# Operands, modulation and result additions moved in a one-core diffusion layer

## The chip, the cores and the metric

The kernel runs on 1 of the 8 cores of a Trainium2 chip. The metric is the device time of one execution in microseconds (us), lower is better. Of the kernel before there are three timed runs, and one further execution was recorded by the hardware profiler.

## The reference

One layer on 1024 latent tokens and 256 context tokens of width 1024. All is float32.

```python
x  = x  + 0.5 * ml[2] * swiglu(modulate(rms_norm(x,  norm1_g), ml[0], ml[1]), ffn1_w_in, ffn1_w_out)
cx = cx + 0.5 * mc[2] * swiglu(modulate(rms_norm(cx, norm1_g), mc[0], mc[1]), ffn1_w_in, ffn1_w_out)
hx = modulate(rms_norm(x, norm2_g), ml[3], ml[4])
hc = modulate(rms_norm(cx, norm2_g), mc[3], mc[4])
bg, cg, vc, q, k, v, gate = split(hx @ w_in)       # hc @ w_in gives keys and values of the context
y  = bg * short_conv(cg * vc, conv_w)
o  = attention(rope(norm(q)), [k_c, rope(k)], [v_c, v])
x  = x + ml[5] * ((sigmoid(gate_c) * (y @ w_bc) + sigmoid(gate_a) * (o @ w_ba)) @ w_out)
x  = x + 0.5 * ml[8] * swiglu(modulate(rms_norm(x, norm3_g), ml[6], ml[7]), ffn2_w_in, ffn2_w_out)
out = rms_norm(x, final_g)
```

The nine modulations are `ml = split(silu(c) @ w_mod + b_mod)`, and `mc` likewise from `c_ctx`. Each is a vector of 1024 numbers that needs 4 MB of `w_mod`. Modulation 5 scales the mixers' result, 6 and 7 shift and scale the third norm, and 8 scales the second FFN's result. From the fifth on only the latent ones are needed.

## The kernel before

**Numbers in two parts.** Every operand of a large product is split into a high part (ScalarE, ACT, casts it) and a low part (VectorE, DVE, subtracts the high part from the original). A product is then three matmuls: high by high, high by low, low by high (`split`, `mm3`, `terms`). So each tile of an operand costs one cast and one subtraction before TensorE (PE) can use it.

**Seven products for eight.** The large products run by Winograd's variant of Strassen's scheme. In `Winograd`, products 1, 2, 6, 7, 4, 5 and 3 are made for a pair of weight column blocks, and DVE combines their results. Each product is 12 matmuls of 128x512. Its right operands are eight sets `r[0..7]`, made from the two token halves by the norm. `norm0` makes the sets of the first half, and `norm1` makes sets 6 and 5 channel by channel and at its end keeps sets 7, 4 and 3, four casts and four subtractions each. `start` makes products 1 and 2 of the first nine pairs ahead, and `run(norm, ...)` in between draws the norm's steps. What is left of the norm is put into `self.late`, and `second` draws from it.

**Rows.** `row_products` does the FFNs' second halves in the same scheme, in the order 2, 1, 4, 6, 5, 7, 3. One product is 11 blocks of hidden rows in groups of two, each block 12 matmuls into four PSUM banks. Products 1, 6 and 7 accumulate in the same four banks (`chain`). `sums` forms the combined operands of later products behind each group, `add` (`add1`, `add3`) puts a finished product's results onto the tokens, and `after1` and `after3` are called behind each group and at the end of a product: they store the tokens, take their squares and draw steps of the next norm (`norms2`). The second FFN's last product is done in two halves of the tokens (`halves=True`).

**Modulations.** The first ones are made at the start. `later_mod` makes the others on DVE from `w_mod`: for each half of a modulation it has eight loads of 256 KB, each followed by a multiply-add into an accumulator for every stream (latent, context). Some empty steps follow, then the split of the accumulator, some more steps, and two matmuls with a column of ones that sum over the partitions. ACT copies the row, four small DMAs turn it into a column, and DVE adds the bias. It is a generator: each `yield` is a step, and the loops around it draw steps. `STEPS` says how many are drawn behind each of the first FFN's 22 column blocks, with three more for each of 12 blocks of context work at the 12th; the rest of `steps` follows at the end of that loop. `late_steps` (modulations 6, 7 and 8) are drawn in the mixers and in the second FFN.

**Mixers and merge.** The mixers loop over eight channel blocks. Each has one pair for `cg` and `vc` and one for `bg` and `gate_c`, and every second has one for `gate_a`. Then come the keys, values and queries, the attention, and the merge: `merge(j, ch)` is 24 matmuls for a block of 128 output channels and half of the tokens, 14 of them behind the attention. The product with `w_out` follows, and the second FFN.

**Order of the work.** The program is traced in order, and a scheduler then orders each engine's queue by its own estimate of when things are ready, with the earlier traced first among those that are. An instruction that is pinned (`keep_in_program_order`) stays behind the one traced just before it on its engine. Everything issued while `strict[0]` is true is pinned. The unpinned may move past it. Each engine then works its queue in the order that was fixed. Loads and stores go through the queue of SP, and a few accumulating loads through that of POOL. Small tiles of 128x512 (`ttile`, tag "t") share eleven buffers: accumulators, loaded rows of `w_mod`, sums of weights on POOL, the mixers' values, squares, head values. An instruction that needs one waits until the last user of an older one is done.

Nearly all instructions are issued by the helper in line 88, so the profile is read by the tiles' names: `r` right operands, `wl` and `wh` weights in parts, `s` sums of weights, `macc`, `acch` and `accl` a modulation's accumulator and its parts, `rawm` the rows of `w_mod`, `uc` values made ahead, `x` tokens, `hid` the FFN's hidden rows, `ga` and `z` the merge's operands, `oh` and `ol` the attention's output in parts, `xb` and `hsw` head values.

## Time and profile before

| what | value |
|---|---|
| three runs, median (lowest to highest) | 2687.64 us (2686.28 to 2688.88) |
| the profiled execution, its own time | 2688.7 us |
| its span, first to last instruction | 2686.9 us |
| mean granted TensorE clock | 0.993 |
| DVE busy | 2007.1 us (75%) |
| ACT busy | 1166.1 us (43%) |
| moved by DMA | 364.84 MB, mean 136 GB/s |

The span is the time between the first and the last instruction of the program in the trace, and 1.8 us of the execution lie around it. An engine's busy time is the union of its instructions. TensorE's matmuls overlap in the records, so its busy time says where it had nothing to do and not how fast it went; the number of matmuls in a stretch says that. The granted clock is what the throttle let TensorE have.

The work lies as follows on the span's axis: the first FFN's first half from the start to 671 us, its second half to 887, the mixers to 1287, heads and attention to 1840, the merge to 1933, the product with `w_out` to 2021, and the second FFN to the end.

### The profile page before, as it was taken

The page shows a single profiled execution, that of the slowest core. Times are in us where ns is not written, and L with a number is a line of the kernel's source. Part 1 is how long each engine was busy: PE and PEld are TensorE (multiplying, and loading weights), DVE is VectorE, ACT ScalarE, POOL GpSimd, SP SyncE. Part 2 cuts the span into 40 slices and gives each one's busy share as a digit, 9 for nine tenths or more (in the row PEclk, how much of TensorE's full clock was granted, in tenths as well). Part 3 has the DMA queues.
Part 4 walks back from the last instruction along what each step waited for, and adds up shares of the span by engine and source line. Part 5 has one row for each costly group of instructions (what it writes and reads, how often), then busy time and mean ns, then how long its engine had stood idle before and what let it go on. Part 6 is the DMA issues. An engine that isn't in the chain of part 4 may idle for free.

```text
span 2686.9 us, 37399 instructions
## 1 busy us (share of the span) xinstructions
PE 2643.4 (98%) x13593; PEld 2236.0 (83%) x13593; DVE 2007.1 (75%) x3356; ACT 1166.1 (43%) x2317; POOL 521.3 (19%) x409
## 2 busy tenths in 40 slices
PE   8999999999999999999999999999999999999998
PEld 5788898888788877888999888877888888888888
DVE  5888888786887889877488666775458875667875
ACT  6633543333454632333244666674236333334543
POOL 1244012121110044232033111000001533230200
PEclk9999999999999999999999999999999999999998
DMA  7655653346973445433213211002524543228731
GB/s 267 236 180 166 223 184 124 109 130 240 293 169 102 149 137 165 134 114 116 97 48 103 95 62 49 24 25 78 167 85 146 184 145 99 83 90 305 165 83 63
DMA packets 369920, 364.84 MB, mean 136 GB/s; under 512 B 27830, under 2 KB 261448, under 8 KB 369736
## 3 DMA queue, kind: packets, MB, share of 16 engines
q1 hardware_dynamic: 360712, 345.17, 39.0%
q0 software_dynamic: 9024, 17.30, 4.0%
q8 instruction: 106, 1.74, 0.3%
q14 instruction: 78, 0.64, 0.1%
HBM read 296.30 MB, written 66.06 MB: 135 GB/s over the span
## 4 chain that ended last, share of the span: by engine, by line
PE 88%; DVE 6%; DMA 2%; ACT 2%; issue 1%; SPq 1%; POOL 0%; DVEq 0%; ACTq 0%; POOLq 0%
PE ps L88 73%; PE po L88 7%; PE pt L88 7%; DMA rawm<-in_w_mod_dram 1%; DVE macc L88 1%; DVE wl L88 1%; SPq L88 1%; DVE xb L88 0%; DVE r L88 0%; ACT r L88 0%; DMA raw<-in_ffn_w_in_dram 0%; DMA xtok<-in_ctx_dram 0%; DVE ol L88 0%; DVE x L88 0%; DVE pts L88 0%
## 5 line engine op out<-in xcount | busy, mean ns | idle before, releaser
L88 PE MATMUL ps<-r,wl 128*128 128x512 f32 x5232 | 1213.4, 392 | 11.6 <-ACT wl L88 6.8
L88 PEld LDWEIGHTS ps<-r,wl 128*128 128x128 f32 x5232 | 983.9, 189 | 220.0 <-ACT wl L88 9.0
L88 ACT CAST wl<-s 128x512 fp32r<-128x512 f32 x256 | 158.0, 620 | 338.3 <-PE ps L88 266.6
L88 POOL TENSOR_TENSOR s<-raw 128x512 f32<-128x512 f32 x64 | 92.4, 1444 | 993.8 <-PE ps L88 346.6
L88 ACT CAST wl<-raw 128x512 fp32r<-128x512 f32 x286 | 176.4, 619 | 250.0 <-PE ps L88 160.6
L88 DVE TENSOR_TENSOR wl<-raw,wl 128x512 fp32r<-128x512 f32 x284 | 202.6, 717 | 68.3 <-ACT wl L88 64.7
L88 DVE TENSOR_TENSOR wl<-s,wl 128x512 fp32r<-128x512 f32 x256 | 231.8, 906 | 12.3 <-ACT wl L88 10.7
L88 POOL TENSOR_TENSOR s<-raw,s 128x512 f32<-128x512 f32 x64 | 99.8, 1560 | 363.9 <-DVE wl L88 354.4
L88 DVE SCALAR_TENSOR_TENSOR macc<-rawm,silu_c,macc 128x512 f32<-128x512 f32 x168 | 137.9, 837 | 9.5 <-DMA rawm<-in_w_mod_dram 9.1
L88 PE MATMUL ps<-wh,r 128*128 128x256 f32 x768 | 141.6, 285 | 0.0
L88 DVE TENSOR_TENSOR pts<-pt,pts 128x512 fp32r<-128x512 f32 x160 | 108.8, 687 | 39.4 <-ACT pts L88 38.4
L88 DVE TENSOR_TENSOR u<-u,ps 128x512 f32<-128x512 f32 x168 | 114.2, 680 | 28.5 <-PE ps L88 28.4
L88 DVE TENSOR_REDUCE m<-ps 128x1 f32<-128x512 f32 (+1 forms) x192 | 110.9, 596 | 31.0 <-PE ps L88 30.3
L88 ACT CAST pts<-pt 128x512 fp32r<-128x512 f32 x160 | 93.2, 593 | 88.7 <-PE pt L88 86.8
L88 ACT CAST rh<-hid 128x512 fp32r<-128x512 f32 x132 | 81.6, 621 | 112.2 <-PE ps L88 96.2
L88 PE MATMUL ps<-rh,wl 128*128 128x512 f32 x360 | 122.0, 389 | 0.0
L88 PEld LDWEIGHTS ps<-wh,r 128*128 128x128 f32 x768 | 120.6, 192 | 0.0
L88 ACT CAST wh<-raw 128x512 fp32r<-128x512 f32 (+1 forms) x88 | 69.3, 795 | 103.0 <-PE ps L88 79.5
L88 PE MATMUL po<-pts,vh 128*128 128x512 f32 x256 | 110.5, 437 | 1.5 <-ACT pts L88 1.5
L88 DVE TENSOR_TENSOR rl<-hid,rh 128x512 fp32r<-128x512 f32 x132 | 90.1, 686 | 26.5 <-ACT rh L88 13.5
L88 PE MATMUL ps<-wl,r 128*128 128x256 f32 x384 | 108.8, 283 | 0.0
L88 PE MATMUL ps<-kl,qs 128*128 128x512 f32 x384 | 105.3, 397 | 0.0
(298 smaller groups left out, 5068.1 us busy)
## 6 DMA issues: line engine op xcount, KB each, us to landing
raw<-in_ffn_w_in_dram SPq DMA_DIRECT2D x125, 512.0 KB
raw<-in_ffn_w_out_dram SPq DMA_DIRECT2D x72, 512.0 KB
rawm<-in_w_mod_dram SPq DMA_DIRECT2D x128, 256.0 KB
raw<-in_w_in_dram SPq DMA_DIRECT2D x61, 512.0 KB
hid<-hd SPq DMA_DIRECT2D x40, 512.0 KB
ws<-in_ffn_w_out_dram POOLq DMA_DIRECT2D x30, 512.0 KB, 6.6
ucd<-uc SPq DMA_DIRECT2D x22, 512.0 KB
hd<-c SPq DMA_DIRECT2D x38, 256.0 KB
```

Of the source, the lines that this page charges most:

```text
L88: inst = getattr(self.engine, name)(*args, **kw)
```

## The change

- **Late operands.** In the mixers' `start`, no norm step is drawn at pairs 5, 6 and 8, so operand sets 4 and 3 are still to be made when it ends. `second` makes set 4 between products 6 and 7 and set 3 behind product 4, both pinned. The line that drew `9 - self.n_ahead` steps is removed; with nine pairs made ahead it drew none.
- **Modulations.** Modulation 5 moves from the first FFN's steps to `late_steps`. These are drawn two at a time in the mixers from the fourth channel block on (30 in all, before 78), five behind each of the 14 merges (70), and the rest in the second FFN (28, before 36). The first FFN draws 154 steps in all, before 198. In `later_mod` each stream's split is followed by three steps and its own matmuls; before, all streams were split, and six steps later all were multiplied. A half of one stream has 16 steps, before 19.
- **Results.** In `row_products` a product's results are added behind the first group of the next product, pinned (unpinned in the second FFN's halves), and the call at the end of a product moves with them. Two steps of the mixers' first norm move a group later, from groups 0 and 4 to 2 and 6.

```diff
-STEPS = (0, 4, 4, 4, 5, 5, 5, 5, 5, 5, 5, 2, 12)
+STEPS = (0, 3, 3, 4, 4, 4, 4, 4, 4, 4, 4, 4, 7)
...
-            parts = []
-            for acc in accs:
+            for acc, v in zip(accs, streams):
                 ah, al = ttile("acch", dt=F32R), ttile("accl", dt=F32R)
                 split(acc, ah, al)
-                parts.append((ah, al))
-            for _ in range(6):
-                yield
-            for (ah, al), v in zip(parts, streams):
+                for _ in range(3):
+                    yield
                 mod, pm = (modl, modc)[v], ps_t()
...
-                run(norm, 2 if i == 0 else 1)
+                run(norm, 2 if i == 0 else 0 if self.plain and i in (5, 6, 8) else 1)
...
-            run(norm, 9 - self.n_ahead)
...
-            run(self.late, 4)
+            self.late_operands(1)
             dve.tensor_add(out=v, in0=u, in1=self.product(7))
...
-            run(self.late)
+            self.late_operands()
             return v, b
+
+        def late_operands(self, n=None):
+            strict[0] = True
+            run(self.late, n)
+            strict[0] = False
...
-        chain = None
+        chain, results = None, []
+
+        def add_results():
+            while results:
+                i, ps = results.pop()
+                for o, ch in to[i]:
+                    for d in range(4):
+                        add(o + d, ch, ps[d])
+                after(i, rows.n)
+
...
                 strict[0] = True
                 sums(i, g)
+                add_results()
                 strict[0] = False
                 after(i, k)
-            for o, ch in to[i]:
-                for d in range(4):
-                    add(o + d, ch, ps[d])
-            after(i, rows.n)
+            results.append((i, ps))
+        if not halves:
+            add_results()
...
                     kept.append(lr)
+                add_results()
                 after(8, k)
...
-        for m in range(2, 6):
+        for m in range(2, 5):
             yield from later_mod(m)
 
-    steps, late_steps = all_later_mods(), (step for m in (6, 7, 8) for step in later_mod(m))
+    steps, late_steps = all_later_mods(), (step for m in (5, 6, 7, 8) for step in later_mod(m))
...
-        if i == 3 and k in (0, 4):
+        if i == 3 and k in (2, 6):
             run(norms2, 1)
...
-        if i > 1:
-            run(late_steps, 5)
+        if i > 2:
+            run(late_steps, 2)
         for ch, bg, gc in mixed():
-            if i > 1:
-                run(late_steps, 4)
+            if i > 2:
+                run(late_steps, 2)
...
                 run(merge(j, ch))
+                run(late_steps, 5)
```

## The prediction

> **What bounds the kernel now.** I read the page first, then the stretches by stage, then TensorE's waits and the timelines around its gaps.
>
> ```profile
> span 2686.9 us, 37399 instructions
> PE 2643.4 (98%) x13593; PEld 2236.0 (83%) x13593; DVE 2007.1 (75%) x3356; ACT 1166.1 (43%) x2317; POOL 521.3 (19%) x409
> PE   8999999999999999999999999999999999999998
> ```
>
> TensorE is busy from end to end, and the change neither adds nor removes a matmul. So a gain can only come out of its gaps and of the time its clock was lowered. The stretches say where these lie: us, TensorE busy (matmuls), weight loads, DVE, ACT, POOL, granted clock, DMA.
>
> ```profile
> 680.00:720.00 40.00, 36.94 (x168) 30.14 (x167) 34.12 (x48) 17.75 (x31) 5.03 (x4) 1.00 0.98 317
> 720.00:930.00 210.00, 210.00 (x948) 174.45 (x947) 173.13 (x275) 108.80 (x186) 16.66 (x15) 1.00 0.54 143
> 930.00:960.00 30.00, 24.95 (x98) 20.09 (x97) 24.95 (x41) 16.80 (x34) 13.39 (x8) 0.89 0.46 150
> 1050.00:1070.00 20.00, 17.43 (x64) 13.47 (x63) 19.59 (x28) 4.93 (x9) 9.43 (x7) 0.83 0.34 110
> 1290.00:1450.00 160.00, 160.00 (x1324) 159.06 (x1324) 105.82 (x289) 65.66 (x236) 37.21 (x72) 1.00 0.19 62
> 1840.00:1930.00 90.00, 90.00 (x408) 74.55 (x407) 45.78 (x62) 22.78 (x32) 0.00 (x0) 1.00 0.43 134
> 2110.00:2410.00 300.00, 300.00 (x1325) 247.95 (x1324) 202.72 (x279) 96.08 (x160) 100.44 (x69) 1.00 0.36 113
> 2410.00:2600.00 190.00, 190.00 (x840) 157.34 (x839) 157.77 (x224) 88.63 (x154) 26.66 (x22) 1.00 0.71 197
> ```
>
> The row of 2110 is undisturbed 512-wide work: 300 / 1325 = 0.2264 us a matmul. At that rate 930:960 lost 30 - 98 x 0.2264 = 7.8 us and 1050:1070 lost 20 - 64 x 0.2264 = 5.5 us, in both with a lowered clock (0.89, 0.83). In 680:720 there are shorter matmuls too, so I take its gaps. TensorE's timeline has them, the time in brackets being idle time:
>
> ```profile
> 703.11 0.50 PE L88 MATMUL pt<-rh,wl 128*128 128x512 f32 x1 [1.39 <-ACT wl L88]
> 706.92 0.73 PE L88 MATMUL pt<-rh,wl 128*128 128x512 f32 x2 [1.67 <-DVE wl L88]
> 943.57 2.93 PE L88 MATMUL ps<-r,wl 128*128 128x512 f32 x6 [5.05 <-ACT wl L88]
> 1057.68 0.73 PE L88 MATMUL ps<-r,wl 128*128 128x512 f32 x2 [1.51 <-ACT wl L88]
> 1059.48 2.93 PE L88 MATMUL ps<-r,wl 128*128 128x512 f32 x6 [1.07 <-DVE wl L88]
> ```
>
> Three places: the turn from the first to the second product of the first FFN's output (3.06 us idle), the start of the mixers (7.8), and the mixers' ninth pair (5.5). Each one is a part of the change. Together they are 16.4 us, or 0.6% of the span. That is the ceiling of what its aims can bring.
>
> **Results a group later.** `row_products` traced the additions of a product right behind its last matmul. DVE and ACT at that turn:
>
> ```profile
> 702.44 0.62 ACT L88 CAST wl<-raw 128x512 fp32r<-128x512 f32 x1 [0.29 <-DMA raw<-in_ffn_w_out_dram]
> 701.81 2.72 DVE L88 SCALAR_TENSOR_TENSOR x<-ps,gate_l,x 128x512 f32<-128x512 f32 x4
> 704.45 1.21 DVE L88 TENSOR_TENSOR hid<-hid,hid 128x1024 f32<-128x1024 f32 x1
> 706.18 0.68 DVE L88 TENSOR_TENSOR wl<-raw,wl 128x512 fp32r<-128x512 f32 x1
> ```
>
> The first gap (1.39) ends with ACT's high part of a weight that had just landed: the DMA engines are 0.98 busy there, and the change leaves those bytes, so I leave this gap. The second ends with the low part. DVE could have made it at 703.1, but four additions (2.72 us) and a sum (1.21 us) stood ahead of it. With the additions traced behind the first group's operands this gap goes: -1.7 us. Ends: 0 (the weight's other half is late too) and -3.06. No bank is missed: the next product but one is the first to want the delayed banks, and it is a whole product away. At the later turns, in both FFNs, there is no gap to win: TensorE is busy in 210.00 of 210 us and in 190.00 of 190.
>
> Behind the seventh product more is moved: its eight additions, SP's eight stores, ACT's squares, the root for the next norm, now all pinned, and two norm steps a group later (24 matmuls, 5.4 us). What that norm feeds:
>
> ```profile
> 878.41 4.88 DVE L88 TENSOR_TENSOR x<-x,pt 128x512 f32<-128x512 f32 x8 [0.53 <-PE pt L88]
> 885.61 0.74 DVE L88 SCALAR_TENSOR_TENSOR x<-ps,gate_l,x 128x512 f32<-128x512 f32 x1
> ```
>
> It ends barely ahead of the mixers' first product, which begins about when the last results appear (885.61). If its time slid with its place, TensorE would wait up to 5.4 us. But it ran far behind its old place in the program already, held up by squares that were mixed with operands. Pinned, the squares come first, so I take 0; ends: -1 (a residue at 943 less) and +5.4.
>
> **Late operands.** Ahead of the 5.05 us gap:
>
> ```profile
> 936.17 3.74 ACT L88 CAST r<-t 128x512 fp32r<-128x512 f32 x7
> 940.29 0.62 ACT L88 CAST r<-t 128x512 fp32r<-128x512 f32 x1
> 940.82 2.18 ACT L88 CAST r<-h 128x512 fp32r<-128x512 f32 x4
> 942.89 1.14 ACT L88 CAST wl<-s 128x512 fp32r<-128x512 f32 x2
> 934.51 1.74 POOL L88 TENSOR_TENSOR s<-raw,raw 128x512 f32<-128x512 f32 x1
> 937.93 4.29 DVE L88 TENSOR_TENSOR r<-t,r 128x512 fp32r<-128x512 f32 x7
> 943.34 2.48 DVE L88 TENSOR_TENSOR r<-h,r 128x512 fp32r<-128x512 f32 x4
> ```
>
> POOL's weight sums are there at 936.3, yet ACT casts them at 942.89, behind twelve casts of right operands (eight of them r<-t). The change makes eight of the twelve, those of products 4 and 3, inside the first pair. Then ACT has four left, 4 x 3.74/7 = 2.1 us, and the weights come about 4.3 us sooner, sooner still if the norm ran ahead. TensorE went idle at 943.57 - 5.05 = 938.5 and needs a weight's low part two matmuls later, at about 939. DVE has 4 x 4.29/7 = 2.5 us of the four that stay, until 940.4, and then the low part, 0.7 us as at 706.18. So a residue of 0 to 2.1 us stays; I take 1.0, and the sum has -6.8 here. The eight that moved cost DVE 8 x 0.61 = 4.9 us in the pair's 60 matmuls (13.6 us). They are pinned behind the addition of product 6 and the subtraction of product 4, with the later additions and weight low parts of the same pair queued behind them; who waits are products 4 and 3, each a product (12 x 0.2264 = 2.7 us) or more away, with four weights made ahead. That covers it; were the cover gone, it would cost up to 2.5 us.
>
> The clock gives the residue another price. At 943 a 5.05 us gap came with 0.89 over 30 us, 3.3 us of clock; at 1057 two gaps of 1.51 and 1.07 came with 0.83 over 20 us, 3.4 us; 1.39 and 1.67 at 703 came with 1.00. So a residue of 2.1 may or may not bring some 3.3 us more: upper end 5.4. In the Trainium skill, "TensorE: Matmul & The Clock Gate", section "Why this matters for your kernels", the clock falls after idle gaps above about 3 us. By that rule the residue would cost itself alone, and the sum would be the same with 3.3 us off its upper end; the trace at 1057 disagrees, since neither gap there reaches 3 us.
>
> **Modulations.** At 1057 the chain is one of buffers:
>
> ```profile
> 1053.04 1.47 POOL L88 TENSOR_TENSOR s<-raw 128x512 f32<-128x512 f32 x1 [10.38 <-DVE accl L88]
> 1055.60 1.37 POOL L88 TENSOR_TENSOR s<-s,raw 128x512 f32<-128x512 f32 x1 [1.09 <-DMA yd<-y]
> ```
>
> POOL had data but no tile among the eleven of "t": a modulation's accumulator held one until DVE's low part. The change starts the late modulations at the fourth channel block instead of the third, two steps a time for four or five, so the first split moves to the sixth block, where no set-aside pair is fetched into these tiles any more. I take the whole 5.5; ends 0 (the same at the new place) and -5.5.
>
> In the merge 14 x 5 = 70 steps are added, at 16 a half 4.4 halves. Durations of one step (min/median/max):
>
> ```profile
> L88 DVE SCALAR_TENSOR_TENSOR macc<-rawm,silu_c,macc x168: 737/745/1821, 30.4 to 2212.2; 128x512 f32<-128x512 f32 x168
> L88 DVE TENSOR_SCALAR macc<-rawm,silu_c x24: 472/484/1524, 29.4 to 2173.2; 128x512 f32<-128x512 f32 x24
> L88 DVE TENSOR_TENSOR accl<-macc,acch x24: 679/684/1782, 42.7 to 2231.3; 128x512 fp32r<-128x512 f32 x24
> SPq L88 <- DVE wl L88: 68.2, 11, 45.0
> ```
>
> A half is 7 x 0.745 + 0.484 + 0.684 = 6.4 us of DVE, so 28 us on the 45.8 of 90: covered. POOL is empty there. On SP each half puts eight loads of 256 KB and four small ones ahead of the merge's weights, about 9.2 MB in 90 us or 102 GB/s on 134, under the 317 shown above. SP's own waits there are for weight buffers (68.2 us, last row), so it runs ahead. If a load holds SP for want of a tile, TensorE pays: 0 to 5.5 us by the row at 1050; I take 0.5, nearest to the idle DVE. In the first FFN two halves leave (12.8 us of DVE) from stretches without gaps: 0. Its other order could move the 1.13 and 1.80 us gaps below, hence -2.9 as an end. In the second FFN 28 steps stay of 36, beside full TensorE: 0.
>
> ```profile
> 277.32 0.39 PE L88 MATMUL ps<-h1ch,wl 128*128 128x256 f32 x1 [1.13 <-ACT wl L88]
> 287.43 0.51 PE L88 MATMUL ps<-h1ch,wl 128*128 128x256 f32 x2 [1.80 <-DVE wl L88]
> ```
>
> **Sum.** The profiled execution took 2688.7 us, 1.1 above the runs' median of 2687.64. 2688.7 - 1.7 - 6.8 - 5.5 + 0.5 = 2675.2; less 1.1: 2674.
>
> **Rivals.** One halving of the clock stays. With the mixers' start unchanged it is 2688.7 - 1.7 - 5.5 + 0.5 - 1.1 = 2680.9; with the ninth pair unchanged 2679.6. For it: the tile shortage is only moved to another block. Against: there the fetched pairs are gone.
>
> The stalls move. All work stays, DVE is 19.59 of 20 us busy at 1050, and the scheduler orders everything unpinned anew; what leaves the start is paid in the first pair, the split of the sixth block starves POOL as the third did. Time: 2687. Against: the waits were for order and buffers, not for DVE's throughput. Nor need the change do what it says: outside the mixers the late operands are none (both other starts use their norm up), so that edit acts once only.
>
> Slower: a tile held too long. The last mixer step is the 30th; the second half is split at its 29th step and multiplied at its 32nd, which stands behind the first full merge. So two of eleven "t" tiles stay taken from about 1290 to 1840, through eleven head projections. Against it: heads need four, two and two at a time by the code, and TensorE is 160.00 of 160 busy with ACT at 65.66. The price, if nine do not do: a starved POOL cost 5.5 us at 1050. Four such events, 22 us, give 2674 + 22 = 2696; from three on the gain is gone.
>
> **How the numbers follow.** A measurement of this kernel can tell about 0.2%, 5.4 us, from no change. Forecast 0.60; one halving stays 0.13; stalls move 0.15; slower 0.12. Faster: 0.60 and most of 0.13, 0.71; same 0.17; slower 0.12. The low end is all three places and the two early gaps gone: 2688.7 - 16.4 - 2.9 - 1.1 = 2668. The high end takes in the unchanged case, 2687; outside lie the slower case and a little below.
>
> **What would show it.** Right: no matmul with over 1 us of idle time near 703-707 behind DVE, near 938-944 or in the mixers; clock 1.00 between 700 and 1300; r<-h casts behind the first pair's product 4; macc rows beside oh matmuls with TensorE full. Wrong: a gap before the mixers' first product, POOL rows waiting for accl again, gaps in head projections, or PE waits on acch or accl in the merge.

## The result, and the profile after

The kernel after takes 2698.34 us (median of six runs, 2693.71 to 2699.97), the kernel before 2686.73 us in the six runs beside it. The ratio is 1.0042 with a 95% interval of 1.0029 to 1.0055. So the change makes the kernel slower by 0.42%, or 11.6 us, where 13.6 us of gain were forecast. The profiled execution took 2698.92 us, 10.2 more than that of before.

The page of the kernel after has the same matmuls, and less work on DVE:

```profile
span 2696.9 us, 37342 instructions
PE 2648.1 (98%) x13593; PEld 2236.1 (83%) x13593; DVE 2000.3 (74%) x3356; ACT 1167.5 (43%) x2317; POOL 523.0 (19%) x409
```

The stretches of the kernel after that answer to those shown of before (us, TensorE busy and its matmuls, weight loads, DVE, ACT, POOL, granted clock, DMA share, GB/s):

```profile
650.00:690.00 40.00, 32.78 (x158) 26.22 (x157) 23.84 (x39) 13.09 (x25) 0.00 (x0) 0.87 0.95 348
680.00:720.00 40.00, 38.82 (x159) 31.73 (x159) 28.89 (x49) 17.65 (x32) 3.81 (x3) 0.91 0.93 289
930.00:960.00 30.00, 28.10 (x123) 22.48 (x122) 26.66 (x42) 16.48 (x30) 12.89 (x7) 1.00 0.59 192
1050.00:1070.00 20.00, 20.00 (x90) 16.56 (x89) 19.10 (x29) 5.09 (x10) 11.66 (x7) 1.00 0.51 161
1290.00:1450.00 160.00, 160.00 (x1317) 158.72 (x1316) 107.13 (x292) 67.23 (x238) 39.12 (x75) 1.00 0.18 57
1450.00:1530.00 80.00, 75.49 (x381) 61.74 (x379) 47.77 (x96) 41.39 (x98) 14.96 (x13) 1.00 0.31 97
1930.00:1960.00 30.00, 26.62 (x110) 20.95 (x109) 21.49 (x33) 5.99 (x9) 0.00 (x0) 0.94 0.75 242
```

Three of them need a row of the kernel before that the prediction did not show, because nothing was lost there:

```profile
650.00:690.00 40.00, 39.65 (x209) 33.77 (x207) 28.60 (x48) 15.09 (x27) 0.00 (x0) 1.00 0.95 356
1450.00:1530.00 80.00, 79.89 (x410) 66.67 (x409) 51.79 (x107) 46.54 (x109) 18.50 (x16) 1.00 0.32 103
1930.00:1960.00 30.00, 30.00 (x134) 24.84 (x133) 11.71 (x13) 5.90 (x7) 0.00 (x0) 1.00 0.58 194
```

Read the pairs. The mixers' ninth pair (1050:1070) is full now and their start (930:960) nearly so: these gains came. But three places that were full have holes: the start of the first FFN's rows (650:690, clock 0.87), the start of the attention (1450:1530), and the way from the merge to the output projection (1930:1960).

For all runs I worked out one more figure from the trace: the TensorE time lost in a stretch, that is the time from the start of each matmul to the start of the next, less what this takes in undisturbed work (0.227 us with 512 columns, 0.120 with 256, and so on). It counts gaps and a lowered clock alike. In us of one profiled execution each:

| kernel | 650-700, rows start | 700-750, turn | 900-1000, mixers start | 1000-1100, ninth pair | 1450-1600, attention | 1900-2000, merge | elsewhere | sum |
|---|---|---|---|---|---|---|---|---|
| before | 0.8 | 3.6 | 8.2 | 5.9 | 3.8 | -0.1 | 45.1 | 67.3 |
| after | 12.2 | -0.1 | 4.8 | -0.1 | 8.8 | 6.2 | 45.9 | 77.8 |
| results alone | 0.8 | 3.7 | 8.1 | 6.0 | 3.7 | -0.1 | 45.8 | 68.0 |
| operands alone | 0.7 | 3.7 | 4.5 | 6.5 | 4.2 | -0.1 | 41.3 | 60.8 |
| modulation alone | 12.0 | -0.1 | 9.9 | -0.1 | 9.4 | 7.2 | 46.2 | 84.4 |
| nine steps | 1.9 | 3.6 | 4.6 | 0.1 | 8.7 | 7.1 | 43.3 | 69.3 |
| nine steps, again | 1.9 | 3.7 | 4.5 | -0.1 | 9.2 | 7.8 | 47.5 | 74.5 |
| modulation 5 done | 11.7 | -0.1 | 6.5 | -0.1 | 4.2 | 0.0 | 51.9 | 74.0 |
| no merge draws | 1.9 | 3.6 | 4.8 | 3.5 | 3.8 | -0.1 | 43.0 | 60.6 |

From before to after that is +11.4 - 3.7 - 3.4 - 6.0 + 5.0 + 6.3 + 0.8 = 10.4 us, the 10.2 us between the two profiled executions. The two lines of the nine steps are one kernel in two executions: their sums differ by 5 us, so a difference of that size in the sums of two single profiles decides nothing, while the columns of the places repeat within 0.7 us.

### The profile page after: what moved, and what is told of

It reads as the page before. It is cut to its first block, busy times and chain, and to the rows that moved or that the text cites. A ratio compares the mean times of both kernels' runs of the same rounds, so it can differ in the third digit from the quotient of the medians.

```text
span 2696.9 us, 37342 instructions
## 1 busy us (share of the span) xinstructions
PE 2648.1 (98%) x13593; PEld 2236.1 (83%) x13593; DVE 2000.3 (74%) x3356; ACT 1167.5 (43%) x2317; POOL 523.0 (19%) x409
## 4 chain that ended last, share of the span: by engine, by line
PE 88%; DVE 6%; DMA 2%; ACT 2%; issue 1%; SPq 0%; POOL 0%; DVEq 0%; ACTq 0%; POOLq 0%
PE ps L88 73%; PE po L88 8%; PE pt L88 7%; DMA raw<-in_ffn_w_in_dram 1%; DVE r L88 1%; DVE wl L88 1%; DVE xb L88 0%; DMA rawm<-in_w_mod_dram 0%; SPq L88 0%; DMA x<-xd 0%; DMA zd<-g 0%; DVE pts L88 0%; DVE macc L88 0%; DVE t L88 0%; DVE y L88 0%
## 5 line engine op out<-in xcount | busy, mean ns | idle before, releaser
L88 DVE TENSOR_TENSOR wl<-s,wl 128x512 fp32r<-128x512 f32 x256 | 217.9, 852 | 20.9 <-ACT wl L88 18.8
L88 DVE SCALAR_TENSOR_TENSOR macc<-rawm,silu_c,macc 128x512 f32<-128x512 f32 x168 | 140.0, 847 | 10.3 <-DMA rawm<-in_w_mod_dram 9.9
L88 PE MATMUL ps<-rh,wh 128*128 128x512 f32 x300 | 102.5, 390 | 0.0
```

What stands on the lines that cost most here:

```text
L88: inst = getattr(self.engine, name)(*args, **kw)
```

## The experiments

**The three parts one by one.** The first four runs apply lines of the diff to the kernel before: `add_results` and the later `norms2` alone; `late_operands` and the shorter `start` alone; `STEPS`, `later_mod` and the draws of `late_steps` alone; and the first two together.

> The kernel before with the results of a product added a group later (and the two calls of the second norm moved to the later groups), nothing else. Theory A, that the loss comes from where the steps of the modulation were put and that the other two parts gain: the two gaps at the turn from the first to the second product of the first FFN's rows (3.6 us of TensorE time in the profile before, none after) go, nothing else changes, 2683 us, ratio 0.9987 (0.9980 to 0.9995). Rival B, that the pinned additions and operands cost: the 11.5 us lost between 650 and 700 us after, where the rows begin, belong to this part, and the run is at 2691 us or above (1.0015 or more). Rival C, that the scheduler lays the whole program out anew at any edit and no part has a size of its own: the gaps before the mixers and at 1450 to 2000 us change too, by several us in either direction.

> The kernel before with the late operands of the mixers (pinned, and three steps of the norm moved out of the start) alone. Theory A: the start of the mixers at 938 to 950 us falls from 8.2 us of lost TensorE time to some 2.4 as in the profile after, a gap of 1 to 2 us comes some 45 us later, the ninth pair at 1050 to 1070 us keeps its 6 us, everything else as before: 2682 us, ratio 0.9985 (0.9975 to 0.9992). Rival B: pinned operands stall the engines that make them, and the ratio is 1.001 or above. Rival C as for the first run: changes of several us far from the mixers.

> The kernel before with the modulation's edits alone: fewer steps in the first FFN, the two streams split one after the other, modulation 5 drawn in the mixers, five steps after each merge. Theory A: all the losses of the profile after are here (end of the first FFN +11.5 us, its middle +2.2, start of the attention +6, merge to output projection +6.2) and one of the gains (ninth pair of the mixers -6): 2686.7 + 20 = 2706 us, ratio 1.0074 (1.005 to 1.009). Rival B: without the pinned results and operands the modulation costs little, the ninth pair's 6 us show, and the ratio is 0.998 to 1.001. Rival C: a ratio between, with gaps at new places.

> The kernel after with the modulation's edits undone: results a group later and late operands together. Theory A: the sum of the first two runs, 2686.7 - 3.6 - 4 to 6 = 2677 to 2679 us, ratio 0.997 (0.996 to 0.9982). Rival B: slower than before, 1.001 or above. Rival C: not the sum of the first two runs, by more than 4 us.

Measured: results alone 2686.44 us, ratio 1.0002 (0.9994 to 1.0011); operands alone 2685.72 us, 0.9995 (0.9986 to 1.0004); modulation alone 2706.15 us, 1.0071 (1.0056 to 1.0086); the first two together 2684.10 us, 0.9994 (0.9985 to 1.0002). So the modulation's edits carry the whole loss, at the size that theory A gave (2706). The other two parts gain nothing that this measurement can tell; theory A had expected 4 to 10 us of them.

The later results gain nothing at the turn. With them alone, TensorE's gaps there stay (1.81 and 1.26 us, before 1.39 and 1.67), and DVE's and ACT's rows of that run say why:

```profile
704.26 0.50 PE L88 MATMUL pt<-rh,wl 128*128 128x512 f32 x1 [1.81 <-ACT wl L88]
707.65 0.74 PE L88 MATMUL pt<-rh,wl 128*128 128x512 f32 x2 [1.26 <-DVE wl L88]
702.54 2.72 DVE L88 SCALAR_TENSOR_TENSOR x<-ps,gate_l,x 128x512 f32<-128x512 f32 x4
706.91 0.68 DVE L88 TENSOR_TENSOR wl<-raw,wl 128x512 fp32r<-128x512 f32 x1
703.59 0.62 ACT L88 CAST wl<-raw 128x512 fp32r<-128x512 f32 x1 [0.71 <-DMA raw<-in_ffn_w_out_dram]
```

The four additions still run ahead of the weights' low part. By the code, the edit orders them against other pinned work only, the operands of the next group are not pinned, and the scheduler places by readiness: the additions have their data, while the weights have just landed. Yet the run with the modulation alone has no gap at the turn, without the later results. The gaps went because the second product began 11.1 us later than before (714.23 in the kernel after, 703.11 before), while ACT's first cast there that waits for one of its weights came only 6.4 us later (708.82 against 702.44).

The late operands act as forecast at the mixers' start, 8.2 to 2.7 us between 900 and 950, but 1.9 us of it come back near 985, in a gap that waits for DVE wl. The two modulation rows of the table say the rest: 11 us at the rows' start, 5.6 in the attention, 7 in the merge, and the ninth pair's gain of 6 also belong to this part.

**The end of the first FFN.** In the kernel after, the loop draws 148 of the 154 steps of `steps`. The last loads of modulation 4 come out on SP at 666, and its pinned multiplications stand on TensorE between the last context block and the rows:

```profile
672.70 1.69 PE L88 MATMUL po<-hidc,wo 128*128 128x256 f32 x12 [0.78 <-DVE cacc L88]
675.33 0.40 PE L88 MATMUL pt<-acch,ones_r 128*1 128x512 f32 x1 [0.95 <-ACT acch L88]
677.14 0.59 PE L88 MATMUL pt<-accl,ones_r 128*1 128x512 f32 x1 [1.42 <-DVE accl L88]
678.91 0.58 PE L88 MATMUL pt<-acch,ones_r 128*1 128x512 f32 x1 [1.18 <-ACT acch L88]
681.41 2.08 PE L88 MATMUL ps<-rh,wl 128*128 128x512 f32 x4 [1.18 <-ACT rh L88]
```

Each link (split, multiplication, copy of the row, next split) is a gap of about 1 us, and only then come ACT's casts of the rows' first operands. With three gaps of 0.78 us for the context's sums (`cacc`) ahead of them, of which the first row is the last, TensorE is idle 7.1 of the 12.2 us lost; most of the rest goes with the lowered clock of 650:690 (0.87). Experiment:

```
-STEPS = (0, 3, 3, 4, 4, 4, 4, 4, 4, 4, 4, 4, 7)
+STEPS = (0, 3, 3, 4, 4, 4, 4, 4, 4, 4, 4, 4, 9)
```

> The kernel after with nine steps instead of seven for each of the last ten column blocks of the first FFN, so that the loop draws 168 of the 154 steps that there are and none is left for its end. Theory A: the 12.2 us lost between 650 and 700 us go, since no split, no matmul and no load of modulation 4 stands behind the last blocks; but the rows then begin as early as before, and the two gaps at the turn to the second product (3.6 us), which the run with the modulation alone does not have and the run with the later results alone still has, come back, because the right-hand blocks' loads land at the same time as before. 2698.3 - 11.5 + 3.6 = 2690.4 us, ratio to the kernel before 1.0014 (1.000 to 1.0025). Rival B: the stall comes from the rows' own loads on SP and half of it or more stays, ratio 1.002 or above. Rival D: the later results do take the gaps at the turn away once the rows begin on time, 2686.8 us, ratio 1.000 or below.

> The kernel with nine steps for each of the last ten column blocks, once more, for a second profile. If the nine steps gain what the first profile shows, 650 to 710 us loses 5.6 us as there (12.2 in the profile after) and the spread lies elsewhere, between 1440 and 1560 us or between 1900 and 2000 us; if not, 650 to 700 us loses up to 12 us again. 2690 to 2700 us.

Measured: the loss at the rows' start goes (12.2 to 1.9 us), and the gaps at the turn come back, 3.6 us as theory A said:

```profile
702.67 0.50 PE L88 MATMUL pt<-rh,wl 128*128 128x512 f32 x1 [1.23 <-ACT wl L88]
706.64 0.72 PE L88 MATMUL pt<-rh,wl 128*128 128x512 f32 x2 [1.86 <-DVE wl L88]
```

That is 6.6 us net, in both profiles. But the timed runs do not show it: 2698.57 us, ratio 1.0043 (1.0031 to 1.0055), as the kernel after. The profiled execution, at 2690.84 us, was the fastest of six; the second took 2695.95. So by profile the cause at this place is shown, and its net worth in the time of this kernel, taken alone, is open. (With modulation 5 done as well it does show; see the runs that put the steps elsewhere.)

**The tiles of modulation 5.** Its second half is split on ACT at 1261.42 in the kernel after, and multiplied at 1873.10. Two of the eleven "t" tiles are held in between. ACT and TensorE at the start of the attention:

```profile
1261.42 0.61 ACT L88 CAST acch<-macc 128x512 fp32r<-128x512 f32 x1
1873.10 0.40 PE L88 MATMUL pt<-acch,ones_r 128*1 128x512 f32 x1
1462.51 0.62 ACT L88 CAST qs<-q 128x512 fp32r<-128x512 f32 x1 [7.16 <-DMA zd<-g]
1466.04 0.62 PE L88 MATMUL ps<-kc,qs 128*128 128x256 f32 x3 [2.29 <-ACT pc L88]
1516.02 0.62 ACT L88 CAST qs<-q 128x512 fp32r<-128x512 f32 x1 [3.35 <-DMA zd<-g]
```

The cast of qs waits for a tile that the store of g gives back, and ACT's exponentials (pc) stand behind it. Before, that wait was 2.46 us. Experiment:

```
+    run(late_steps, 2)
     for k in range(4):
         mix.part_second(k)
```

> The kernel after with two more steps of the modulation after the mixers' loop, so that the second half of modulation 5 is multiplied at the mixers' end and not behind the first full merge, and its two t tiles are not held through the projections and the attention. Theory A: ACT's stands at a cast of qs for a t tile that a store of g must free (7.2 and 3.4 us in the profile after, 2.5 before) shrink, and the gaps near 1466 and 1518 us (2.3 and 2.0 us, some 6 us of TensorE time with what they bring) go: 2692 us, ratio to the kernel before 1.0020 (1.001 to 1.003). Rival B: the tiles are not short for that reason, the gaps stay within 2 us, ratio 1.0035 or above.

Measured: 2694.54 us, ratio 1.0027 (1.0017 to 1.0038). The attention's loss falls from 8.8 to 4.2 us (3.8 before), so the held tiles are the cause there. The run with two more tiles, further below, agrees: the attention's loss is 5.0 us in it, against 10.3 with the same steps and eleven tiles. The merge's 6.2 us went too, which nobody had expected: all later steps now fall two earlier. And 4.9 us came new between 1750 and 1850; their cause was not looked for.

**The merge.** I first took the last gaps for loads of ga that stand on SP behind the output projection's weights, and moved the same 70 steps to the first ten merges:

```
-                run(late_steps, 5)
+                run(late_steps, 7 if j < 6 else 0)
```

> The kernel after with seven steps of the modulation after each of the first ten merges and none after the last four, 70 in all as after. Theory A: the last merges' loads of ga no longer stand on SP behind the load of the output projection's weights, which waits 9.6 us for its buffer, and the gaps near 1946 and 1953 us (6.2 us lost in all between 1900 and 2000) go: 2692.3 us, ratio to the kernel before 1.0021 (1.001 to 1.003). Rival B: the ga loads are late because the merges themselves are, and the seven steps make them later: the same gaps or larger, ratio 1.004 or above.

> The kernel after with all three edits: nine steps in the first FFN's last blocks, modulation 5 done at the mixers' end, seven steps after the first ten merges. Theory A: the sum, 2698.3 - 7.9 - 6 - 6 = 2678.4 us, ratio to the kernel before 0.9969 (0.9955 to 0.9982), that is before less the 3.7 us that the late operands gain and the 6 us of the mixers' ninth pair, and a little for the two steps that are left wrong in the first FFN's middle. Rival C: the three are not independent and the sum is missed by over 4 us.

Both failed. 2724.07 us, ratio 1.0136 (1.0123 to 1.0149), and all three edits together 2697.23 us, 1.0040 (1.0028 to 1.0052), of which 14.4 us are lost in the merge. The run with seven steps lost 29.5 us there, and its rows show another chain, from TensorE through ACT and SP back to TensorE:

```profile
1917.28 0.40 PE L88 MATMUL pt<-accl,ones_r 128*1 128x512 f32 x1
1918.01 0.57 ACT L88 COPY mrow<-pt 1x512 f32<-1x512 f32 x1
1918.60 2.41 SPq L88 DMA_DIRECT2D mcol<-mrow  x4
1921.11 0.54 SPq L88 DMA_DIRECT2D ga<-gad  x1
1924.34 0.69 DVE L88 TENSOR_TENSOR ga<-ga,ps 128x512 f32<-128x512 f32 x1 [1.59 <-DMA ga<-gad]
1925.08 0.80 PE L88 MATMUL ps<-oh,wh 128*128 128x512 f32 x1 [7.41 <-DVE ga L88]
```

The row of a modulation is multiplied at the end of a merge, where its matmul is pinned. SP's four copies of the row wait for it (SP stood 30.2 us for ACT mrow between 1880 and 1985 us), the loads of ga and z stand behind them in the queue, and the merges' results wait for ga. Six runs took this chain apart, all with the seven steps except the second:

```
-                    sp.dma_start(out=mcol[:, j : j + 1], in_=row[:1, j * P : (j + 1) * P])
+                    act.dma_start(out=mcol[:, j : j + 1], in_=row[:1, j * P : (j + 1) * P])
```

(copies on ACT's queue),

```
-                run(merge(j, ch))
+                step = merge(j, ch)
+                run(step, 1)
                 run(late_steps, 7 if j < 6 else 0)
+                run(step)
```

(loads first),

```
-A_BUFS = 38
+A_BUFS = 37
...
-    tpool = ctx.enter_context(tc.tile_pool(name="tpool", bufs=11))
+    tpool = ctx.enter_context(tc.tile_pool(name="tpool", bufs=13))
```

(two more tiles of tag "t", one of the larger A tiles fewer), the first and the third of these together, and

```
             for acc, v in zip(accs, streams):
+                if m > 5:
+                    for _ in range(3):
+                        yield
+                    c0 = m * 8 + half * 4
+                    dve.tensor_add(out=modl[:, c0 : c0 + 4], in0=acc[:, :4], in1=bcol[:, c0 : c0 + 4])
+                    continue
```

(the rows of modulations 6 to 8 left out, so that the kernel's result is another one).

> The run with seven steps after each of the first ten merges lost 29.5 us of TensorE time between 1900 and 2000 us, in gaps of 7.4, 6.8 and 7.9 us that waited for ga; SP stood 30.2 us in four waits for ACT mrow between 1880 and 1985 us, the longest 9.4. Here the same kernel issues the four copies of each row of the modulation (mcol from mrow) on ACT's queue in place of SP's, nothing else. Theory E: in the merges the copy of a row waits on SP for a row that TensorE makes only after a whole merge, and the loads of ga and z for the next merge stand behind it in SP's queue; then the three gaps go, and the time falls from 2724 to 2695-2700 us, ratio to the kernel before 1.003 to 1.0055. Rival: the ga loads are late for want of t tiles or of DMA time, and the gaps stay: 2715 us or above, ratio 1.0105 or more.

> The run before this one with the copies of the rows (mcol from mrow) on ACT's queue as well. Theory E: no load of the merges stands behind a copy that waits for a row, the merges' gaps are gone whatever the phase, and so is the jitter of several us between executions: 2680 to 2684 us, ratio to the kernel before 0.9975 to 0.9993. Rival: the copies now stand in ACT's queue and hold its casts, as casts waiting for t tiles do in the attention, and the ratio is that of the run before this one or above.

> The run with seven steps after each of the first ten merges, but with the seven steps drawn behind the first part of the next merge, so that its loads of ga and z stand ahead of them in the program; as many steps, loads and merges as there. Theory F: the loads of ga and z are late only because they stand in SP's queue behind loads of the modulation that wait for t tiles; then the 29.5 us lost between 1900 and 2000 us fall below 10, and the time to 2700 us or below, ratio to the kernel before 1.0055 or less. Rival: the ga loads themselves wait for t tiles, which the modulation's loads hold wherever they stand, or the scheduler puts them back; the loss stays above 20 us, ratio 1.010 or above.

> The run with seven steps after each of the first ten merges, with 13 t tiles in place of 11 (and 37 A tiles in place of 38, which may bring waits elsewhere). Theory F: with two more tiles SP's waits for tiles freed by DVE macc between 1880 and 1985 us shrink and the 29.5 us lost between 1900 and 2000 us fall by half or more; the gaps at the attention's start, which wait for a t tile too, shrink as well: 2700 to 2708 us, ratio to the kernel before 1.005 to 1.0085. Rival: the copies of the rows hold SP just as long (30.2 us there), and the loss between 1900 and 2000 us stays above 20 us.

> The run with seven steps after each of the first ten merges, with the rows of modulations 6 to 8 left out: no split, no multiplication with ones, no copy of the row, the columns are made from the accumulator's first four columns instead, so that the output is another one; all loads, all accumulations and the number of steps stay. Theory G: each half of a modulation that ends among the merges costs one round trip (last matmul of a merge, copy of the row, four copies on SP, and only then the loads of ga and z), three in the run before, 7 us each; without rows there is none, the loss between 1900 and 2000 us falls from 29.5 to below 8 us and the time to 2700 us or below, ratio to the kernel before 1.0055 or less. Rival: the 70 loads and accumulations hold the tiles and SP by themselves, the loss stays above 15 us, ratio 1.008 or above.

> The run with seven steps after each of the first ten merges, with the row copies on ACT's queue and 13 t tiles (37 A tiles) together. Theory G': row copies and tiles each hold SP when the other does not, so that only both together free it: loss between 1900 and 2000 us below 10 us (29.5, 23.3 and 29.3 with none or one of the two), 2700 us or below, ratio 1.0055 or less. Rival: DVE and ACT themselves stand in order behind the modulation's loads (ACT stood 9.3 us at a cast of mh that followed a split waiting for a load), and the loss stays above 15 us, ratio 1.008 or above.

Measured, with the loss between 1900 and 2000 us: copies on ACT's queue 2723.50 us, 1.0142 (1.0126 to 1.0157), 23.3 us lost; loads of ga ahead of the draws 2720.40 us, 1.0123 (1.0103 to 1.0143), 25.8 us; two more tiles 2720.44 us, 1.0131 (1.0118 to 1.0145), 29.3 us; copies and tiles together 2714.24 us, 1.0103 (1.0088 to 1.0118), 16.8 us; rows left out 2689.52 us, 1.0014 (1.0004 to 1.0023), nothing lost. The run with copies on ACT's queue without the seven steps took 2690.18 us, 1.0017 (1.0009 to 1.0026), no better than without that edit, so there was nothing for it to win. Of the five runs with seven steps, the rival came true in all but the one with the rows left out. The stretch 1880:1985 of three runs: first with seven steps, then with copies and tiles, then with the rows left out.

```profile
1880.00:1985.00 105.00, 82.71 (x334) 65.61 (x334) 62.57 (x94) 20.73 (x29) 0.00 (x0) 0.89 0.69 227
```

```profile
1880.00:1985.00 105.00, 95.42 (x391) 76.02 (x390) 69.62 (x103) 23.23 (x33) 0.00 (x0) 0.93 0.72 232
```

```profile
1880.00:1985.00 105.00, 105.00 (x465) 86.95 (x464) 69.81 (x102) 22.54 (x27) 0.00 (x0) 1.00 0.78 261
```

The last one answers it. With all 70 loads and all accumulations in place (DMA 261 GB/s, the most of the three; DVE 69.81 of 105) TensorE is full. So with seven steps what costs is not the bytes and not DVE's accumulations but the row: the split with its two tiles, a matmul pinned behind a merge, and the copies, which wait in three queues one after the other. That last run takes all of these out together and does not tell them apart. The queues take each other's place as holder: with the copies alone moved to ACT's queue, SP waits for tiles instead, some of them tiles of rows that their copies give back.

```profile
SPq L88 <- DVE macc L88: 33.9, 11, 10.8
SPq L88 <- DMA mcol<-mrow: 11.9, 7, 5.0
```

With both edits 16.8 us are still lost, and SP is not free of the rows: it waits 23.4 us for such tiles and 16.0 us for weight buffers between 1880 and 1985. Which of these holds TensorE was not tried.

In the kernel after itself, with five steps, it is not the row. Its last gaps follow a load of ga that SP issued right behind two loads of the output projection's weights, for whose buffer it had stood 9.1 us, as I had first taken it:

```profile
1930.57 9.96 SPq L88 DMA_DIRECT2D raw<-in_w_out_dram  x2
1940.58 0.57 SPq L88 DMA_DIRECT2D ga<-gad  x1
1941.74 2.57 SPq L88 DMA_DIRECT2D mcol<-mrow  x4
1944.99 0.69 DVE L88 TENSOR_TENSOR ga<-ga,ps 128x512 f32<-128x512 f32 x1 [4.87 <-DMA ga<-gad]
1945.73 0.50 PE L88 MATMUL ps<-mh,wh 128*128 128x512 f32 x1 [3.17 <-DVE ga L88]
```

The row's copies stand behind that load, and between 1880 and 1985 SP waited only 2.2 us for rows. In the run with modulation 5 done it waited 12.8 us for rows in that stretch and nothing was lost, since all loads of ga but the last stand ahead of those weights:

```profile
1939.58 0.32 SPq L88 DMA_DIRECT2D ga<-gad  x1
1940.76 7.08 SPq L88 DMA_DIRECT2D raw<-in_w_out_dram  x2
```

The other profiles with five steps a merge fall the same way: modulation alone and both of the nine steps, with four loads of ga behind the weights, lose 7.1 to 7.8 us, and nine steps with modulation 5 done, with one behind, loses nothing. So the order of these loads on SP is what goes with the 6.3 us; no run changed that order alone.

**Putting the steps elsewhere.** Three runs ask whether the placement is all: nine steps with modulation 5 done; the same with the 70 steps in the head projections (`run(late_steps, 6)` after each unit); and no draws in the merge, but more in the mixers from the third round on:

```
-        if i > 2:
-            run(late_steps, 2)
+        if i > 1:
+            run(late_steps, 6)
...
-            if i > 2:
-                run(late_steps, 2)
+            if i > 1:
+                run(late_steps, 5)
...
-                run(late_steps, 5)
```

> The kernel after with nine steps in the first FFN's last blocks and modulation 5 done at the mixers' end, the merges left as they are (five steps after each). Theory A: each gains what its own profile showed (8.4 and 3.7 us of TensorE time), 2698.3 - 12 = 2686 us, ratio to the kernel before 1.000 (0.999 to 1.0015). Theory E, that the merges' gaps hang on where a row's copy falls on SP and move with every shift of the steps: with 32 steps done at the merges' start, as with modulation 5 done alone, the last merges lose nothing and the ratio is 0.998 to 1.000. Rival: the run with nine steps alone was timed at 2698.6 us although its profiled execution took 2690.8, so the nine steps gain nothing in most executions: 2694.5 us, ratio 1.003.

> The kernel after with nine steps in the first FFN's last blocks, modulation 5 done at the mixers' end, no steps after the merges, and six steps after each of the eleven units of the head projections in their place. Theory: the steps cost nothing where no load that TensorE needs soon stands behind theirs; no loss between 1900 and 2000 us, none at the ninth pair, the attention as before, the turn's 3.6 us back: 2677 to 2682 us, ratio to the kernel before 0.9965 to 0.9985. Rival: the head projections need the t tiles and SP (weights of 1 MB a unit), gaps of several us come between 1060 and 1450 us, ratio 1.000 or above.

> The kernel after with nine steps in the first FFN's last blocks and with no steps after the merges: instead 16 in each of the mixers' last six rounds (six, five, five), where the kernel before draws 13, so that modulations 5, 6 and 7 are done at the mixers' end. Theory A and E: no loss between 1900 and 2000 us (6.2 us after), none at the start of the attention (6 us), which leaves the ninth pair: if its 6 us come from the steps drawn in the third and fourth rounds, they come back, and the time is 2698.3 - 8 - 6 - 6 + 6 = 2684 us, ratio to the kernel before 0.9993 (0.998 to 1.0005); if they come from the old order of the splits, they stay away, and it is 2678 us, ratio 0.997. Rival: the mixers' tiles run short in more pairs, and the ratio is 1.002 or above.

Measured: nine steps with modulation 5 done 2688.68 us, 1.0009 (1.0000 to 1.0018), with no loss in the merge; against modulation 5 done without the nine steps (1.0027) that is 0.18%, or about 5 us of the 6.6 that the profiles gave them; steps in the heads 2695.56 us, 1.0038 (1.0025 to 1.0050), where 2677 to 2682 us were expected, since the last unit's rotation (DVE xb) comes late and leaves TensorE idle for 5.83 us ahead of 1460, with 14.7 us in the attention's column in all; no merge draws 2685.39 us, 0.9999 (0.9991 to 1.0008). The last one bears on the ninth pair's 6 us:

```profile
1047.14 1.29 POOL L88 TENSOR_TENSOR s<-raw 128x512 f32<-128x512 f32 x1 [5.64 <-DMA gcd<-v]
1051.73 1.44 POOL L88 TENSOR_TENSOR s<-s,raw 128x512 f32<-128x512 f32 x1 [3.31 <-DMA yd<-y]
1053.87 0.73 PE L88 MATMUL ps<-r,wl 128*128 128x512 f32 x2 [0.58 <-ACT wl L88]
1055.46 6.87 PE L88 MATMUL ps<-r,wl 128*128 128x512 f32 x29 [0.85 <-DVE wl L88]
```

With sixteen steps a round from the third on, the gaps are back, smaller (0.58 and 0.85 us against 1.51 and 1.07), and without the lowered clock that made some 3 of before's 5.9 us: 1.9 us are lost at these gaps, 3.5 in the whole column. So steps drawn in the third and fourth rounds bring gaps there. POOL is short of tiles again, but they come back from stores (of v and y), and none of POOL's rows there waits for accl. Whether the old order of the splits made a part of the 6 us no run shows. With the steps out of the way of the rows, of the attention and of the merge, the 11.6 us are gone and the kernel is as fast as before; no version here is measurably faster than it. That its profile has 6.7 us less lost than before's, and the times no difference, fits a profiled execution that was the fastest of twelve (2681.57 us).

## Why the prediction was wrong

The chance went to "faster" because the steps that move were priced at their new places by the busy time of engines and by a wait seen elsewhere, and in three places what would then stand ahead of what in the queues was not read.

- **"In the first FFN two halves leave (12.8 us of DVE) from stretches without gaps: 0."** This step failed by 11.4 us, the largest term. The halves that leave cost nothing; but the steps drawn per block were cut as well, and the half that remains last slid to the loop's end, where pinned links in series stand ahead of the rows, with a lowered clock behind their gaps. Summing `STEPS` against the steps there are (148 of 154) would have told it. Nine steps take it away (12.2 to 1.9 us).
- **"With the additions traced behind the first group's operands this gap goes: -1.7 us."** It stays in the run with this part alone (1.26 us idle), because the additions stand ahead of the weight's low part as before. It went in the kernel after, with the other gap of the turn, only because the rows began later. The end of 0 was the right one, though its reason, a weight's other half that is late too, is not the one seen.
- **Late operands, -6.8 us.** The mechanism was right and the size was not: 8.2 to 2.4 us at the start, two residues of 0.90 and 1.00 us of idle time, and 2.4 us new between 950 and 1000, most of it one gap at 993.68 (1.54 us idle) for DVE wl. In size that is the cover that was priced at up to 2.5 us and taken as whole; but the gap lies some 45 us behind the mixers' start and not in the first pair, and that DVE's delayed work is what reaches it is argued. The run with the operands alone has such a gap too (1.9 us lost). Net -3.4 us. The norm did not run ahead.
- **Ninth pair, -5.5 us.** Right in size (-6.0 us). The run without merge draws agrees in part: steps in those rounds make tiles short and bring gaps back, at another holder than accl.
- **Merge, "0 to 5.5 us by the row at 1050; I take 0.5, nearest to the idle DVE".** 6.3 us, just past the upper end. What failed is the sentence ahead of it, "SP's own waits there are for weight buffers (68.2 us, last row), so it runs ahead": those waits are the ones that hurt. Before, SP had issued its last load of ga, at 1907.62, when two loads of the output projection's weights took it 11.26 us from 1914.20 on; with the modulation's loads put in, four loads of ga come behind such a pair, which stood 9.1 us for its buffer. DVE's idle time was no price for that. Loads and accumulations by themselves are covered, as said (nothing lost with the rows left out); with seven steps a merge the row, which the step counted only as four small loads, costs more still.
- **The rival "a tile held too long", 0.12.** Its mechanism is real, tiles held from 1261 to 1873, and it decided a part of the sign. Its place was wrong: the head projections stay full (160.00 of 160) and the attention loses 5.0 us. Alone its 5.0 us could not have outweighed the 13.1 us gained elsewhere. That the rival's 2696 us lie near the 2698.34 measured is luck.
- **Stretches that were to stay full** in both FFNs' later products did, and so did the clock between 700 and 1300 us.

## What to carry to other kernels

When work drawn in steps is redistributed, add up the steps against the draws and look at where the last ones fall: a remainder that falls at a loop's end stands in series, whatever it costs in the middle. Price a moved step by its longest chain through the queues and by what the queue it joins already waits for, not by the busy time it adds: here 70 loads and accumulations cost nothing in the merge once the rows were left out, a load of ga behind a weight buffer's wait left TensorE idle for 3.17 us, and a row of 512 numbers behind a pinned matmul for 7.41. And test each part of a change alone, since a gap can vanish for a reason that has nothing to do with the edit aimed at it.

## What the runs showed of the hardware

The same two gaps can bring a lowered clock or not. At the mixers' start the kernel after and the run without the modulation's edits have nearly the same pair, the first in this fence and the other in the second:

```profile
948.39 1.25 PE L88 MATMUL ps<-r,wl 128*128 128x512 f32 x4 [0.90 <-ACT wl L88]
950.65 2.60 PE L88 MATMUL ps<-r,wl 128*128 128x512 f32 x10 [1.00 <-DVE wl L88]
```

```profile
939.74 1.25 PE L88 MATMUL ps<-r,wl 128*128 128x512 f32 x4 [0.89 <-ACT wl L88]
941.99 4.36 PE L88 MATMUL ps<-r,wl 128*128 128x512 f32 x11 [1.01 <-DVE wl L88]
930.00:960.00 30.00, 28.10 (x116) 22.13 (x115) 27.55 (x38) 17.23 (x34) 15.47 (x8) 0.94 0.48 155
```

Ten matmuls take 2.60 us in the one, where the clock of 930:960 is 1.00. In the other eleven take 4.36 us, at a clock of 0.94. So a pair of 0.9 and 1.0 us may cost 1.5 us more (4.36 less 2.60 and one matmul of 0.23) or nothing. The clock's own records in these traces say where such a size comes from: in all twenty profiles the granted clock is either full or half, and every stretch at half clock but the last of a run lasts 3.4 us or a multiple of it. With TensorE busy, 3.4 us at half clock cost 1.7. At the mixers' start the run without the modulation's edits has one such stretch, from 942.0 on; the kernel before has 6.8 us there and again at the ninth pair, and the kernel after 10.2 us at the rows' start. Seven gaps of 0.78 to 1.42 us at the rows' start of the kernel after go with a clock of 0.87. The Trainium skill, "TensorE: Matmul & The Clock Gate", section "Why this matters for your kernels", has the clock fall for idle gaps above about 3 us; no gap in these three places comes near that, so here the measurement decides against it. The same page of the Trainium skill, section "A second HAM failure mode: psum-queue depth-cycling", tells of a kernel whose many short idle times between groups of matmuls make the clock go back and forth; the rows' start agrees with that (0.87), and the pair at the mixers' start does in one run and not in the other.
